# Odd mixer of a two-layer trunk: decay differences and masked U on GpSimd, four gate rows for three

## The chip, the cores and the metric

The kernel runs on one core of a Trainium2 chip, in one launch. The metric is the device time of one execution in microseconds (us). TensorE is PE (PEld its weight loads), VectorE is DVE, ScalarE is ACT, GpSimd is POOL, and SyncE (SP) only issues transfers.

## The reference

One inference step of a two-layer trunk for a prompt of 512 tokens and a sample group of 8 sequences of 4 tokens, width 1024, fp32. Each layer is a half-step FFN, a mixer and another half-step FFN. The mixer of the second (odd) layer is a gated DeltaNet with 8 heads of 128; the change lies in it alone:

```
def deltanet_mixer(u, conv_buf, S0, w_in, conv_w, A_log, dt_bias, o_gain, w_out):
    proj = u @ w_in
    qkv, z, b_logit, a_logit = jnp.split(proj, ...)
    qkv, new_buf = causal_conv(conv_buf, qkv, conv_w)
    q, k, v = jnp.split(jax.nn.silu(qkv), 3, axis=-1)      # q and k are l2-normalized per head
    g = -jnp.exp(A_log) * jax.nn.softplus(a_logit + dt_bias)
    o, S = gated_delta_chunked(q, k, v, beta, g, S0)
    o = rms_norm(o, o_gain) * jax.nn.silu(z)
    return o @ w_out, (new_buf, S)

# in gated_delta_chunked
    G = jnp.cumsum(gc, axis=-1)
    decay = jnp.exp(jnp.where(incl, G[..., :, None] - G[..., None, :], -jnp.inf))
    A = jnp.where(strict, jnp.einsum('bnhcd,bnhsd->bnhcs', kc, kc) * decay, 0.0) * bc[..., None]
```

Then a triangular solve with A, and a scan over the chunks that carries the state S.

## The kernel before

Activations are kept transposed, 128 rows by 544 columns (512 prompt, 32 sample) per tile. Every linear is written by `mm3`: weights and activations are each split in a high and a low part, three products for each of 8 blocks, so 24 matmuls into one PSUM tile `lin` for each half of the columns (256 and 288). In the odd mixer `lin` has two buffers, so PE can be two tiles ahead of the instruction that reads the first one back, which for all of them is one on DVE. A weight block is loaded by SP (`raw`), its high part made on ACT (`wh`, L328) and its low part on DVE (`wl`, L329).

The mixer works on its heads in four groups of two (0 and 1, 2 and 3, 4 and 5, 6 and 7). A string of tokens gives the order in which the pieces are written out, and a scheduler orders each engine's instructions from there; every engine then runs its list strictly in that order. The pieces that matter here:

- **Decays** (`head_decay`): the row G of a head is spread over all partitions by a transfer (`grow` for the first head of a group, the shared tile `xsq` for the second), then `Dn` and `Dt` are made by a subtraction of G per partition and a clamp against a constant mask (L1165, L1166: one DVE instruction per tile and chunk of 128, 16 for a group), and ACT takes the exponentials.
- **Head stage** (`head_stage`): two convolved projections (`conv_tile`: `lin` to `XP` by DVE at L1120, L1123 and L1124, the history columns of XP by POOL, then three DVE instructions `acc` L1134), squares and norms, products. POOL makes `qg` (L1214).
- **Solve**: 62 short DVE instructions `ltmp` (L1251) and `LT` (L1252), each needing the one before.
- **Chain** (`chain`): four chunk steps on PE, ACT and DVE, then `finish`: the norm `fo` by a dozen short DVE instructions (L984 to L989), ACT scales `ot` (L1328), PE transposes it (L1331), DVE multiplies it onto the gate row `sz` (L1335) and splits the result to `y` (L376).
- **Gate** (`gate`): one `mm3` into a row tagged `sz`, read back by DVE at L1565; three rows, one for each head in flight, each free again when `y` is split.
- **Sample state** (`sample_state`): for two heads and two halves of the sequences, `um` is U times a 0/1 mask of each sequence (four ACT instructions, L1518, into one buffer), a matmul `s` (L1520) and four DVE updates of S (L1523).

Rows tagged `st` (15 of them) hold Dn, Dt, kt, qg and vb of the heads in flight. `E.junk` are two scratch tiles for the elementwise result of squares whose sum alone is wanted. The constants `c_tri`, `c_stri` and `c_sones` are loaded once and used in `odd_setup` alone.

Of the kernel before, what the change touches and what calls it, by code (L numbers as in the profile page):

```python
# [7 lines left out]
F32 = mybir.dt.float32  # L8
# [4 lines left out]
ALU = mybir.AluOpType  # L13
# [983 lines left out]
def odd_consts(E, op):  # L997
    nc, I = E.nc, E.I

    def const(key, shape):  # L1000
        t = op.tile(shape, F32, name=key)
        nc.sync.dma_start(out=t, in_=I[key])
        return t
    E.tri = const("c_tri", [P, P])
    E.mba = const("c_mba", [P, P])
    E.mbp = const("c_mbp", [P, P])
    E.stri = const("c_stri", [NS, NS])
    E.sones = const("c_sones", [NS, NS])
    E.smba = const("c_smba", [NS, NS])
    E.smbp = const("c_smbp", [NS, NS])  # L1010
    E.bsel = const("c_bsel", [96, DB])

    rows = E.f(P)[:96]
    nc.sync.dma_start(out=rows, in_=I["dn_conv_w"].rearrange("a i (k p) -> (a i k) p", p=P))
    ps = E.m([P, 96])
    nc.tensor.transpose(ps, rows, E.ident[:96, :96])
    E.cw = op.tile([P, 96], F32, name="cw")
    nc.vector.tensor_copy(E.cw, ps)
    E.cst = op.tile([P, 24, 27], F32, name="dncst")
    cv = I["state_dn_conv"].rearrange("a b i c -> (a b i) c")  # L1020
    for g in range(6):
        st = E.f()
        nc.sync.dma_start(out=st[:24, :512], in_=cv[:, g * 512:(g + 1) * 512])
        ps = E.m([P, 4, 24])
        for j in range(4):
            nc.tensor.transpose(ps[:, j], st[:24, j * P:(j + 1) * P], E.ident[:24, :24])
        nc.vector.tensor_copy(E.cst[:, 4 * g:4 * g + 4, 3:], ps)
    gc = op.tile([P, 1], F32, name="ogain")
    nc.sync.dma_start(out=gc, in_=I["dn_o_gain"].rearrange("a p -> p a"))
    E.ogain = gc  # L1030
    E.ad = op.tile([P, 2, NH], F32, name="ad")
    nc.sync.dma_start(out=E.ad[:, 0], in_=I["dn_A_log"].to_broadcast([P, NH]))
    nc.sync.dma_start(out=E.ad[:, 1], in_=I["dn_dt_bias"].to_broadcast([P, NH]))


def odd_setup(E, op, sp, w_in):
# [5 lines left out]
    def ev(h, c0, cn, ps):  # L1042
        nc.vector.tensor_tensor(bt[:16, c0:c0 + cn], ps[:16], E.rstd[:16, c0:c0 + cn], op=ALU.mult)
    mm3(E, [w], E.xh, E.xl, ev)
    ps = E.m([P, 5, 16])
    for t, (c0, n) in enumerate(TOKS):
# [22 lines left out]
    gf = g[:, :4].rearrange("p a b -> p (a b)")  # L1069
    nc.tensor.matmul(ps[:, 0:32], lhsT=E.tri, rhs=gf, start=True, stop=True)  # L1070
    nc.tensor.matmul(ps[:, 32:64], lhsT=E.ones, rhs=gf, start=True, stop=True)
    nc.tensor.matmul(ps[:NS, 64:72], lhsT=E.stri, rhs=g[:NS, 4], start=True, stop=True)
    nc.tensor.matmul(ps[:NS, 72:80], lhsT=E.sones, rhs=g[:NS, 4], start=True, stop=True)
    nc.tensor.matmul(ps[:, 96:160], lhsT=E.ones[:NS], rhs=gm.rearrange("p a b -> p (a b)"), start=True, stop=True)
# [81 lines left out]
def head_decay(E, op, h):  # L1156
# [5 lines left out]
    Dt = op.tile([P, 4, P], F32, tag="st", name=E.nm("Dt"), bufs=ST)  # L1162
    for c in range(4):
        g = E.G[:, c, h:h + 1]
# [9 lines left out]
def head_stage(E, op, w_in, h, H, ssq, adr, sq):  # L1174
# [5 lines left out]
    kT = conv_tile(E, op, w_in, 1, h, sq)  # L1180
    ssk = op.tile([P, 4], F32, tag="ssk", name=E.nm("ssk"), bufs=2)
    pq = E.m([P, 4, P])
    for c in range(4):
        nc.tensor.transpose(pq[:, c], ch(qT)[:, c], E.ident)
    for c in range(4):
        nc.scalar.activation(E.junk[0], pq[:, c], AF.Square, accum_out=ssq[:, gi, c:c + 1])
    kt = op.tile([P, 4, P], F32, tag="st", name=E.nm("kt"), bufs=ST)
    pk = E.m([P, 4, P])
    for c in range(4):
        nc.tensor.transpose(pk[:, c], ch(kT)[:, c], E.ident)  # L1190
    for c in range(4):
        nc.scalar.activation(E.junk[0], pk[:, c], AF.Square, accum_out=ssk[:, c:c + 1])
    nc.scalar.activation(kt, pk, AF.Copy)
# [115 lines left out]
def chain(E, op, Hs, V, g0, ssq, sz, yy, cuts=(4,)):  # L1309
# [29 lines left out]
    for c in range(4):  # L1339
# [22 lines left out]
        for h in hs:  # L1362
            nc.scalar.activation(E.junk[1], ot[:, c, h], AF.Square, accum_out=sso[:, h, c:c + 1])
        S = Sn
# [31 lines left out]
def sample_group(E, op, sq, dec, g0, sz, yy):  # L1396
# [11 lines left out]
    kt, vt = kv[:, 0], kv[:, 1]  # L1408
    ssk = op.tile([NS, GH], F32, tag="sssk", name=E.nm("ssk"))
    for h in hs:  # L1410
        nc.scalar.activation(E.junk[1][:NS], kt[:, h], AF.Square, accum_out=ssk[:, h:h + 1])
    nc.vector.tensor_scalar(ssk, ssk, EPS, None, op0=ALU.add)
# [30 lines left out]
    nc.vector.tensor_tensor(V, pv, IB, op=ALU.add)  # L1443
    kw = R(P, "kw")
    nc.vector.tensor_tensor(kw, kt, bc(kwf, P), op=ALU.mult)
# [65 lines left out]
def sample_state(E, op, g0, S0, k3, ur):  # L1511
    nc, O = E.nc, E.O
    sp = lambda shape: cps(E, shape, "s")
    for h in range(GH):
        for q in range(2):
            um = op.tile([96, 4, P], F32R, tag="um", name=E.nm("um"))
            for b in range(4):
                nc.scalar.activation(um[:, b], ur[:, h].bitcast(F32), AF.Copy, scale=E.bsel[:, 4 * q + b:4 * q + b + 1])  # L1518
            ps = sp([P, 4, P])
# [7 lines left out]
def odd_mixer(E, cp, w_in, w_out, nxt):  # L1527
    nc, tc = E.nc, E.tc
    with E.phase(0, 2), tc.tile_pool(name=E.nm("oddw"), bufs=1) as op, tc.tile_pool(name=E.nm("odram"), bufs=1, space=bass.MemoryType.DRAM) as dp:
        E.dp, E.op = dp, op  # L1530
        E.ft, E.rt = (op, "acc", XW, 4), (op, "y", YB)
        E.junk = [op.tile([P, P], F32, name=f"junk{i}") for i in range(2)]
        norm_stats(E)
# [4 lines left out]
def odd_heads(E, op, dp, w_in, w_out, nxt):  # L1538
# [18 lines left out]
    def gate(h):  # L1557
        H = st[h // GH * GH]
        E.table("silu_and_others")
        z = op.tile([P, NT], F32, tag="sz", name=E.nm("sz"), bufs=3)  # L1560
        H.sz = getattr(H, "sz", []) + [z]
# [133 lines left out]
```

## Time and profile before

| what | value |
|---|---|
| median of 3 runs | 1911.97 us (1911.93 to 1913.39) |
| profiled execution | 1916.94 us, span 1915.2 us, mean granted clock 0.991 |
| busy: PE, PEld, DVE, ACT, POOL | 97%, 94%, 56%, 44%, 6% of the span |
| odd mixer | about 1198 to 1627 us of the span |

The profiled execution is 4.97 us longer than the median, and its span 1.74 us shorter than itself. Busy shares are means over stages: the odd mixer is read by itself below.

### The profile page before, as it was taken

To read this page: it belongs to the slowest core of one execution; us is meant where nothing else is said; L and a number is where in the kernel's file an instruction comes from. 1 tells how busy PE (TensorE), PEld (TensorE's weight loads), DVE (VectorE), ACT (ScalarE), POOL (GpSimd) and SP (SyncE) were. 2 spreads that over 40 slices of the span, in tenths; PEclk is the share of its full clock that TensorE was granted. 3 is DMA by queue.
4 is the path that set the end of the run, shared out by engine and by line. 5 is a ranking of instruction groups with operands and counts; after the bars stand their busy time and mean duration, and the time that the engine had idled before them with its cause. 6 is when DMAs were issued, how large, how long until landed. Compare 5 with 4: busy or idle time off the path is not lost.

```text
span 1915.2 us, 36694 instructions
## 1 busy us (share of the span) xinstructions
PE 1861.2 (97%) x15101; PEld 1793.0 (94%) x15101; DVE 1078.1 (56%) x2565; ACT 836.9 (44%) x1733; POOL 121.2 (6%) x229
## 2 busy tenths in 40 slices
PE   7999999999999999999999999899998999999999
PEld 6999999889777999999999999799997998999998
DVE  7444335776856444433544433688978877444422
ACT  6333224777755333323333322466675646333221
POOL 0000002111430000000000000111111100000000
PEclk9999999999999999999999999899999999999999
DMA  4323333222431333333332322333343332333232
GB/s 131 86 85 89 87 89 99 76 59 76 141 100 58 89 89 89 89 89 93 90 87 86 88 81 80 87 88 95 99 124 76 94 95 65 89 88 86 81 112 68
DMA packets 315973, 171.05 MB, mean 89 GB/s; under 512 B 28470, under 2 KB 310278, under 8 KB 315804
## 3 DMA queue, kind: packets, MB, share of 16 engines
q1 hardware_dynamic: 313244, 160.30, 29.5%
q0 software_dynamic: 2560, 8.39, 1.5%
q8 instruction: 119, 1.95, 0.4%
q14 instruction: 50, 0.41, 0.1%
HBM read 158.01 MB, written 10.65 MB: 88 GB/s over the span
## 4 chain that ended last, share of the span: by engine, by line
PE 58%; DVE 5%; ACT 2%; issue 1%; DMA 1%; POOL 0%; SPq 0%; ACTq 0%; DVEq 0%; POOLq 0%
PE lin L367 18%; PE lin L368 17%; PE lin L369 17%; DVE acc L1134 1%; DVE wl L329 1%; DVE LT L1252 1%; DVE ltmp L1251 1%; PE s L1479 0%; DMA raw<-in_w_in_odd 0%; PE m L1211 0%; DMA raw<-in_w_ffn_in 0%; ACT wh L328 0%; DVE Dn L1165 0%; PE c L1349 0%; DMA grs<-gdr 0%
## 5 line engine op out<-in xcount | busy, mean ns | idle before, releaser
L367 PE MATMUL lin<-xh,wh 128*128 128x256 f32 (+2 forms) x2992 | 875.0, 293 | 20.0 <-DVE XP L1120 5.0
L368 PE MATMUL lin<-xl,wh 128*128 128x256 f32 (+2 forms) x2992 | 870.5, 291 | 1.4 <-DVE xl L376 0.7
L369 PE MATMUL lin<-xh,wl 128*128 128x256 f32 (+2 forms) x2992 | 865.8, 290 | 0.5 <-DVE wl L329 0.5
L367 PEld LDWEIGHTS lin<-xh,wh 128*128 128x128 f32 (+1 forms) x2992 | 565.6, 189 | 25.7 <-ACT wh L328 6.4
L368 PEld LDWEIGHTS lin<-xl,wh 128*128 128x128 f32 (+1 forms) x2992 | 566.1, 189 | 3.9 <-DVE xl L273 1.5
L369 PEld LDWEIGHTS lin<-xh,wl 128*128 128x128 f32 (+1 forms) x2992 | 566.8, 189 | 2.6 <-issue 0.8
L328 ACT ACTIVATE wh<-raw 128x1024 fp32r<-128x1024 f32 x261 | 275.8, 1057 | 492.1 <-PE lin L368 419.2
L329 DVE TENSOR_TENSOR wl<-raw,wh 128x1024 fp32r<-128x1024 f32 x261 | 317.2, 1215 | 89.9 <-PE lin L369 88.0
L367 PE MATMUL lin<-hh,wh 128*128 128x288 f32 (+1 forms) x1024 | 295.7, 289 | 0.0
L368 PE MATMUL lin<-hl,wh 128*128 128x288 f32 (+1 forms) x1024 | 295.4, 288 | 0.0
L369 PE MATMUL lin<-hh,wl 128*128 128x288 f32 (+1 forms) x1024 | 294.9, 288 | 0.0
L368 PEld LDWEIGHTS lin<-hl,wh 128*128 128x128 f32 x1024 | 193.0, 188 | 0.2
L369 PEld LDWEIGHTS lin<-hh,wl 128*128 128x128 f32 x1024 | 192.7, 188 | 0.1
L367 PEld LDWEIGHTS lin<-hh,wh 128*128 128x128 f32 x1024 | 192.5, 188 | 0.1
L406 DVE TENSOR_TENSOR sg<-lin,rstd 128x256 f32<-128x256 f32 (+1 forms) x128 | 55.9, 438 | 162.1 <-PE lin L369 162.1
L375 ACT ACTIVATE hh<-pr 128x256 fp32r<-128x256 f32 (+1 forms) x128 | 55.1, 431 | 204.1 <-DVE pr L412 203.9
L411 DVE TENSOR_TENSOR pr<-lin,rstd 128x256 f32<-128x256 f32 (+1 forms) x128 | 56.5, 441 | 155.2 <-PE lin L369 155.1
L428 DVE SCALAR_TENSOR_TENSOR x<-lin,x 128x256 f32<-128x256 f32 x64 | 28.2, 441 | 168.7 <-PE lin L369 168.7
L376 DVE TENSOR_TENSOR hl<-pr,hh 128x256 fp32r<-128x256 f32 (+1 forms) x128 | 56.6, 442 | 61.2 <-ACT hh L375 61.2
L100 ACT ACTIVATE sg<-sg 128x256 f32<-128x256 f32 (+1 forms) x128 | 53.7, 422 | 55.9 <-DVE sg L406 55.9
L272 ACT ACTIVATE xh<-x,vec 128x544 fp32r<-128x544 f32 (+2 forms) x64 | 39.6, 631 | 71.5 <-DVE x L428 59.3
L1134 DVE SCALAR_TENSOR_TENSOR acc<-XP,cw,acc 128x568 f32<-128x568 f32 x72 | 58.8, 817 | 2.5 <-ACT acc L1132 2.2
(492 smaller groups left out, 2068.7 us busy)
## 6 DMA issues: line engine op xcount, KB each, us to landing
raw<-in_w_ffn_in SPq DMA_DIRECT2D x128, 512.0 KB
raw<-in_w_ffn_out SPq DMA_DIRECT2D x64, 512.0 KB
raw<-in_w_in_odd SPq DMA_DIRECT2D x32, 512.0 KB
raw<-in_w_in_even SPq DMA_DIRECT2D x20, 512.0 KB
raw<-in_w_out_even SPq DMA_DIRECT2D x8, 512.0 KB
S<-in_state_dn_S SPq DMA_DIRECT2D x8, 512.0 KB
out_dn_S_sample<-S SPq DMA_DIRECT2D x8, 512.0 KB
raw<-in_w_out_odd SPq DMA_DIRECT2D x8, 512.0 KB
```

What stands on the lines that cost most here:

```text
L100: i = self.nc.scalar.activation(out, in_, func, **kw).ins
L272: nc.scalar.activation(xh, x, AF.Copy, scale=g)
L328: nc.scalar.activation(self.h, raw, AF.Copy)
L329: nc.vector.tensor_tensor(self.l, raw, self.h.bitcast(F32), op=ALU.subtract)
L367: nc.tensor.matmul(ps[:n], lhsT=wh, rhs=rh, start=(i == 0), stop=False)
L368: nc.tensor.matmul(ps[:n], lhsT=wh, rhs=rl, start=False, stop=False)
L369: E.last_mm = nc.tensor.matmul(ps[:n], lhsT=wl, rhs=rh, start=False, stop=(i == len(terms) - 1)).ins
L375: nc.scalar.activation(yh, src, AF.Copy)
L376: nc.vector.tensor_tensor(yl, src, yh.bitcast(F32), op=ALU.subtract)
L406: nc.vector.tensor_tensor(s, ps, E.rstd[:, c0:c0 + cn], op=ALU.mult)
L411: nc.vector.tensor_tensor(p_, ps, E.rstd[:, c0:c0 + cn], op=ALU.mult)
L1134: nc.vector.scalar_tensor_tensor(a, XP[:, j:j + XW - 3], cw[j], a, op0=ALU.mult, op1=ALU.add)
```

## The change

- For the heads from 2 on, Dn and Dt are made on POOL: a subtraction of a broadcast G and an addition of a broadcast mask, each over 128x512, four instructions for a head in place of eight on DVE. Heads 0 and 1 stay as they were.
- `um` is one POOL instruction over 96x512 in place of four on ACT.
- The tag `sz` has four rows.
- The scratch tiles are gone: squares write into `kt`, `vb` or `kw`, tiles that are rewritten or no longer read; `kt` of a head and `kw` of the sample are therefore allocated earlier.
- The three constants are loaded in `odd_setup`, by three transfers of SP into a tile tagged `acc`.

```diff
@@ -1001,11 +1001,8 @@
         t = op.tile(shape, F32, name=key)
         nc.sync.dma_start(out=t, in_=I[key])
         return t
-    E.tri = const("c_tri", [P, P])
     E.mba = const("c_mba", [P, P])
     E.mbp = const("c_mbp", [P, P])
-    E.stri = const("c_stri", [NS, NS])
-    E.sones = const("c_sones", [NS, NS])
     E.smba = const("c_smba", [NS, NS])
     E.smbp = const("c_smbp", [NS, NS])
     E.bsel = const("c_bsel", [96, DB])
@@ -1042,6 +1039,10 @@
     def ev(h, c0, cn, ps):
         nc.vector.tensor_tensor(bt[:16, c0:c0 + cn], ps[:16], E.rstd[:16, c0:c0 + cn], op=ALU.mult)
     mm3(E, [w], E.xh, E.xl, ev)
+    cst = E.f()
+    tri, stri, sones = cst[:, :P], cst[:NS, P:P + NS], cst[:NS, P + NS:P + 2 * NS]
+    for t, key in ((tri, "c_tri"), (stri, "c_stri"), (sones, "c_sones")):
+        nc.sync.dma_start(out=t, in_=E.I[key])
     ps = E.m([P, 5, 16])
     for t, (c0, n) in enumerate(TOKS):
         nc.tensor.transpose(ps[:n, t], bt[:16, c0:c0 + n], E.ident[:16, :16])
@@ -1067,10 +1068,10 @@
     nc.vector.tensor_tensor(gm, g[:NS, 4:5].to_broadcast([NS, DB, NH]), bc(E.bsel[:NS], NH), op=ALU.mult)
     ps = E.m([P, 160])
     gf = g[:, :4].rearrange("p a b -> p (a b)")
-    nc.tensor.matmul(ps[:, 0:32], lhsT=E.tri, rhs=gf, start=True, stop=True)
+    nc.tensor.matmul(ps[:, 0:32], lhsT=tri, rhs=gf, start=True, stop=True)
     nc.tensor.matmul(ps[:, 32:64], lhsT=E.ones, rhs=gf, start=True, stop=True)
-    nc.tensor.matmul(ps[:NS, 64:72], lhsT=E.stri, rhs=g[:NS, 4], start=True, stop=True)
-    nc.tensor.matmul(ps[:NS, 72:80], lhsT=E.sones, rhs=g[:NS, 4], start=True, stop=True)
+    nc.tensor.matmul(ps[:NS, 64:72], lhsT=stri, rhs=g[:NS, 4], start=True, stop=True)
+    nc.tensor.matmul(ps[:NS, 72:80], lhsT=sones, rhs=g[:NS, 4], start=True, stop=True)
     nc.tensor.matmul(ps[:, 96:160], lhsT=E.ones[:NS], rhs=gm.rearrange("p a b -> p (a b)"), start=True, stop=True)
     E.G = op.tile([P, 5, NH], F32, name="G")
     nc.vector.memset(E.G, 0.0)
@@ -1160,7 +1161,12 @@
     nc.sync.dma_start(out=grow, in_=E.gdr[h:h + 1].to_broadcast([P, NT]))
     Dn = op.tile([P, 4, P], F32, tag="st", name=E.nm("Dn"), bufs=ST)
     Dt = op.tile([P, 4, P], F32, tag="st", name=E.nm("Dt"), bufs=ST)
-    for c in range(4):
+    if h >= GH:
+        gb = bc(E.G[:, :4, h], P)
+        for d, m in ((Dn, E.mba), (Dt, E.mbp)):
+            nc.gpsimd.tensor_tensor(d, ch(grow), gb, op=ALU.subtract)
+            nc.gpsimd.tensor_tensor(d, d, m.unsqueeze(1).to_broadcast([P, 4, P]), op=ALU.add)
+    for c in range(4 if h < GH else 0):
         g = E.G[:, c, h:h + 1]
         nc.vector.scalar_tensor_tensor(Dn[:, c], ch(grow)[:, c], g, E.mba, op0=ALU.subtract, op1=ALU.max)
         nc.vector.scalar_tensor_tensor(Dt[:, c], ch(grow)[:, c], g, E.mbp, op0=ALU.subtract, op1=ALU.min)
@@ -1179,17 +1185,17 @@
     qT = conv_tile(E, op, w_in, 0, h, sq)
     kT = conv_tile(E, op, w_in, 1, h, sq)
     ssk = op.tile([P, 4], F32, tag="ssk", name=E.nm("ssk"), bufs=2)
+    kt = op.tile([P, 4, P], F32, tag="st", name=E.nm("kt"), bufs=ST)
     pq = E.m([P, 4, P])
     for c in range(4):
         nc.tensor.transpose(pq[:, c], ch(qT)[:, c], E.ident)
     for c in range(4):
-        nc.scalar.activation(E.junk[0], pq[:, c], AF.Square, accum_out=ssq[:, gi, c:c + 1])
-    kt = op.tile([P, 4, P], F32, tag="st", name=E.nm("kt"), bufs=ST)
+        nc.scalar.activation(kt[:, c], pq[:, c], AF.Square, accum_out=ssq[:, gi, c:c + 1])
     pk = E.m([P, 4, P])
     for c in range(4):
         nc.tensor.transpose(pk[:, c], ch(kT)[:, c], E.ident)
     for c in range(4):
-        nc.scalar.activation(E.junk[0], pk[:, c], AF.Square, accum_out=ssk[:, c:c + 1])
+        nc.scalar.activation(kt[:, c], pk[:, c], AF.Square, accum_out=ssk[:, c:c + 1])
     nc.scalar.activation(kt, pk, AF.Copy)
     nc.vector.tensor_scalar(ssk, ssk, EPS, None, op0=ALU.add)
     cf = op.tile([P, 4, 4], F32, tag="cf", name=E.nm("cf"), bufs=4)
@@ -1360,7 +1366,7 @@
             nc.tensor.matmul(po[:, h], lhsT=Hs[h].PT[:, c], rhs=U[:, h], start=(c == 0), stop=True)
         nc.scalar.activation(ot[:, c], po, AF.Copy)
         for h in hs:
-            nc.scalar.activation(E.junk[1], ot[:, c, h], AF.Square, accum_out=sso[:, h, c:c + 1])
+            nc.scalar.activation(Hs[h].vb[:, c], ot[:, c, h], AF.Square, accum_out=sso[:, h, c:c + 1])
         S = Sn
         if c in cuts:
             finish(c - 4 // len(cuts), c)
@@ -1407,8 +1413,9 @@
     nc.scalar.activation(kv, ps, AF.Copy)
     kt, vt = kv[:, 0], kv[:, 1]
     ssk = op.tile([NS, GH], F32, tag="sssk", name=E.nm("ssk"))
+    kw = R(P, "kw")
     for h in hs:
-        nc.scalar.activation(E.junk[1][:NS], kt[:, h], AF.Square, accum_out=ssk[:, h:h + 1])
+        nc.scalar.activation(kw[:, h], kt[:, h], AF.Square, accum_out=ssk[:, h:h + 1])
     nc.vector.tensor_scalar(ssk, ssk, EPS, None, op0=ALU.add)
     cf = op.tile([NS, 4, GH], F32, tag="scf", name=E.nm("scf"))
     rk, rb, rb2, kwf = cf[:, 0], cf[:, 1], cf[:, 2], cf[:, 3]
@@ -1441,7 +1448,6 @@
         nc.tensor.matmul(pv[:, h], lhsT=A2[:, h], rhs=IB[:, h], start=True, stop=True)
     V = R(NS, "V")
     nc.vector.tensor_tensor(V, pv, IB, op=ALU.add)
-    kw = R(P, "kw")
     nc.vector.tensor_tensor(kw, kt, bc(kwf, P), op=ALU.mult)
     k3 = op.tile([96, GH, P], F32R, tag="k3", name=E.nm("k3"))
     for h in hs:
@@ -1514,8 +1520,7 @@
     for h in range(GH):
         for q in range(2):
             um = op.tile([96, 4, P], F32R, tag="um", name=E.nm("um"))
-            for b in range(4):
-                nc.scalar.activation(um[:, b], ur[:, h].bitcast(F32), AF.Copy, scale=E.bsel[:, 4 * q + b:4 * q + b + 1])
+            nc.gpsimd.tensor_tensor(um, ur[:, h].bitcast(F32).unsqueeze(1).to_broadcast([96, 4, P]), bc(E.bsel[:, 4 * q:4 * q + 4], P), op=ALU.mult)
             ps = sp([P, 4, P])
             nc.tensor.matmul(ps, lhsT=k3[:, h], rhs=um, start=True, stop=True)
             s = S0[h][:, 4 * q:4 * q + 4]
@@ -1529,7 +1534,6 @@
     with E.phase(0, 2), tc.tile_pool(name=E.nm("oddw"), bufs=1) as op, tc.tile_pool(name=E.nm("odram"), bufs=1, space=bass.MemoryType.DRAM) as dp:
         E.dp, E.op = dp, op
         E.ft, E.rt = (op, "acc", XW, 4), (op, "y", YB)
-        E.junk = [op.tile([P, P], F32, name=f"junk{i}") for i in range(2)]
         norm_stats(E)
         odd_setup(E, cp, op, w_in)
         odd_heads(E, op, dp, w_in, w_out, nxt)
@@ -1557,7 +1561,7 @@
     def gate(h):
         H = st[h // GH * GH]
         E.table("silu_and_others")
-        z = op.tile([P, NT], F32, tag="sz", name=E.nm("sz"), bufs=3)
+        z = op.tile([P, NT], F32, tag="sz", name=E.nm("sz"), bufs=4)
         H.sz = getattr(H, "sz", []) + [z]
         w = W(E, w_in[:, 3072 + h * P:3072 + (h + 1) * P])
 
```

In all, POOL has 40 instructions more (24 for the decays, 16 for `um`), DVE 48 fewer, ACT 64 fewer.

POOL's list where the decays of heads 2 and 3 are made. `XP` and `dncst` are history columns of the convolutions, `k` belongs to the sample. Before:

```order
L1127 COPY dncst<-XP_13787 128x3 [waits DVE_49]
L1128 COPY dncst<-XP_13787 128x24 [waits DVE_49]
L1115 MEMSET XP_14631 128x3 [waits DVE_49,Activation_49,Pool_49]
L1116 COPY XP_14631<-dncst 128x8x3
L1452 COPY k_1747_14226<-k_1747_14226 32x256 [waits Activation_49,Pool_49]
L1127 COPY dncst<-XP_14560 128x3 [waits DVE_49,Pool_49]
L1128 COPY dncst<-XP_14560 128x24 [waits DVE_49]
```

And now:

```order
L1128 COPY dncst<-XP_13783 128x3 [waits DVE_49]
L1129 COPY dncst<-XP_13783 128x24 [waits DVE_49]
L1116 MEMSET XP_14607 128x3 [waits DVE_49,Activation_49,Pool_49]
L1117 COPY XP_14607<-dncst 128x8x3
L1167 TENSOR_TENSOR Dn_14510<-grow_14508,G 128x512 [waits DMAHW5_49]
L1167 TENSOR_TENSOR Dt_14511<-grow_14508,G 128x512
L1168 TENSOR_TENSOR Dn_14510<-Dn_14510,c_mba 128x512 [waits Pool_49]
L1168 TENSOR_TENSOR Dt_14511<-Dt_14511,c_mbp 128x512 [waits Pool_49]
L1167 TENSOR_TENSOR Dn_14520<-xsq,G 128x512 [waits DMAHW7_49]
L1167 TENSOR_TENSOR Dt_14521<-xsq,G 128x512
L1168 TENSOR_TENSOR Dn_14520<-Dn_14520,c_mba 128x512 [waits Pool_49]
L1168 TENSOR_TENSOR Dt_14521<-Dt_14521,c_mbp 128x512 [waits Pool_49]
```

Eight instructions stand ahead of the history copies of the next projection, and no other engine's result stands between them but the two transfers of G.

DVE's list around the first read-back of the gate row of head 5 (`sz_16595` before, `sz_16543` now; `y_15485` and `y_15487` are the results of heads 2 and 3). Before:

```order
L1335 SCALAR_TENSOR_TENSOR sz_15199<-c_15774,ogain,sz_15199 128x512 [waits PE_49]
L376 TENSOR_TENSOR y_15485<-sz_15138,y_15484 128x512 [waits Activation_49]
L1134 SCALAR_TENSOR_TENSOR acc_16503<-XP_16445,cw,acc_16503 128x568 [waits Activation_49,Pool_49]
L376 TENSOR_TENSOR y_15487<-sz_15199,y_15486 128x512 [waits Activation_49]
L1134 SCALAR_TENSOR_TENSOR acc_16503<-XP_16445,cw,acc_16503 128x568 [waits DVE_49]
L1251 TENSOR_TENSOR ltmp_16522<-LA_16520,LT_16521 128x66
L1134 SCALAR_TENSOR_TENSOR acc_16503<-XP_16445,cw,acc_16503 128x568 [waits DVE_49]
L1252 TENSOR_TENSOR LT_16521<-LT_16521,ltmp_16522 128x22x3 [waits DVE_49]
L1565 TENSOR_TENSOR sz_16595<-lin_16602,rstd 128x256
L1251 TENSOR_TENSOR ltmp_16522<-LA_16520,LT_16521 128x63 [waits DVE_49]
```

And now:

```order
L1260 COPY LA_15236<-LT_15237 128x256 [waits DVE_49]
L1569 TENSOR_TENSOR sz_16326<-lin_16360,rstd 128x288 [waits PE_49]
L329 TENSOR_TENSOR wl_16547<-raw_16544,wh_16546 128x1024 [waits DMAHW0_49]
L1121 TENSOR_TENSOR XP_16393<-lin_16396,rstd 128x256 [waits PE_49,Pool_49]
L1124 TENSOR_TENSOR XP_16393<-lin_16422,rstd 128x256 [waits PE_49]
L1125 TENSOR_TENSOR XP_16393<-lin_16422,rstd 128x8x4
L329 TENSOR_TENSOR wl_16607<-raw_16604,wh_16606 128x1024 [waits DMAHW5_49,Activation_49]
L1283 COPY lv_15312<-c_15319 32x8x32 [waits PE_49]
L1569 TENSOR_TENSOR sz_16543<-lin_16550,rstd 128x256 [waits PE_49]
L1291 COPY lv_15312<-c_15347 32x8x32 [waits PE_49]
```

The gate of head 5 was read back behind the split that frees its row; now it stands among the products of the solve of heads 2 and 3 (`lv`, `V`), ahead of their chain, and its second half follows 55 rows later. On PE the gate's 48 matmuls moved with it: between the last product of that chain (L1360) and the first transposition of its `finish` (L1331) stood 58 matmuls of `lin`, and now stand 40; behind them comes the next group's projection, whose first read-back on DVE stands right behind `fo`.

## Rows read from the trace of the kernel before

**Rows 1.** Stretches: length, busy PE, PEld, DVE, ACT, POOL (instructions), clock, DMA share, GB/s.
```profile
1198.00:1627.00 429.00, 407.41 (x3774) 380.61 (x3772) 347.95 (x1220) 265.48 (x754) 60.93 (x128) 0.97 0.34 91
1275.00:1300.00 25.00, 24.32 (x196) 22.54 (x193) 22.65 (x101) 18.17 (x48) 2.78 (x9) 1.00 0.32 86
1325.00:1350.00 25.00, 24.99 (x211) 24.10 (x209) 23.44 (x93) 23.28 (x84) 4.95 (x9) 1.00 0.46 123
1350.00:1375.00 25.00, 23.73 (x192) 23.08 (x192) 24.07 (x89) 18.29 (x44) 5.21 (x11) 1.00 0.35 96
1425.00:1450.00 25.00, 19.03 (x136) 18.14 (x134) 21.66 (x78) 18.61 (x47) 4.47 (x9) 0.88 0.35 95
```

**Rows 2.** Timeline of PE, 1428 to 1446 us: start, duration, engine, line, operation.
```profile
1428.68 0.39 PE L1360 MATMUL pv<-U,Dt 128*128 128x128 f32 x2
...
1437.38 0.33 PE L1331 MATMUL c<-ident,ot 128*128 128x128 f32 x1 [0.85 <-ACT ot L1328]
...
1440.99 0.27 PE L1405 MATMUL s<-ident,sq 128*32 128x128 f32 x1
1445.78 0.58 PE L367 MATMUL lin<-xh,wh 128*128 128x256 f32 x1 [4.51 <-DVE sz L1565]
```

**Rows 3.** Busy time by engine in 5 us behind that wait.
```profile
1445.00:1450.00 5.00, 4.22 (x20) 4.22 (x20) 4.69 (x17) 2.56 (x8) 0.25 (x2) 0.50 0.17 44
```

**Rows 4.** Timeline of DVE, 1430 to 1446 us.
```profile
1430.40 0.17 DVE L1375 SCALAR_TENSOR_TENSOR sso<-sso,ssq 128x8 f32<-128x8 f32 x1
1431.52 0.35 DVE L1165 SCALAR_TENSOR_TENSOR Dn<-xsq,G,c_mba 128x128 f32<-128x128 f32 x1 [0.96 <-DMA xsq<-gdr]
...
1436.23 0.16 DVE L989 SCALAR_TENSOR_TENSOR fo<-rsa,rsy 128x8 f32<-128x8 f32 x1
...
1442.99 0.68 DVE L376 TENSOR_TENSOR y<-sz,y 128x512 fp32r<-128x512 f32 x1
...
1445.31 0.41 DVE L1565 TENSOR_TENSOR sz<-lin,rstd 128x256 f32<-128x256 f32 x1
```

**Rows 5.** Timeline of PE: two waits, at 1282 and at 1369 us.
```profile
1282.61 0.21 PE L1430 MATMUL s<-ident,sA 32*32 32x32 f32 x2 [0.60 <-DVE ltmp L1251]
...
1369.81 0.39 PE L367 MATMUL lin<-xh,wh 128*128 128x256 f32 x1 [1.27 <-DVE XP L1120]
```

**Rows 6.** Timeline of DVE: two of the decay differences of heads 2 and 3.
```profile
1267.06 0.34 DVE L1165 SCALAR_TENSOR_TENSOR Dn<-grow,G,c_mba 128x128 f32<-128x128 f32 x1
1267.32 0.35 DVE L1166 SCALAR_TENSOR_TENSOR Dt<-grow,G,c_mbp 128x128 f32<-128x128 f32 x1
```

**Rows 7.** Instructions of line 1214: minimum/median/maximum ns, first and last start.
```profile
L1214 POOL TENSOR_TENSOR qg<-acc,grow x4: 1287/1290/1294, 1236.0 to 1503.2; 128x512 f32<-128x512 f32 x4
L1214 POOL TENSOR_TENSOR qg<-acc,xsq x4: 1297/1328/1609, 1254.0 to 1523.1; 128x512 f32<-128x512 f32 x4
```

**Rows 8.** Page, costliest groups: mean ns of one, idle time before them.
```profile
L329 DVE TENSOR_TENSOR wl<-raw,wh 128x1024 fp32r<-128x1024 f32 x261 | 317.2, 1215 | 89.9 <-PE lin L369 88.0
...
L1134 DVE SCALAR_TENSOR_TENSOR acc<-XP,cw,acc 128x568 f32<-128x568 f32 x72 | 58.8, 817 | 2.5 <-ACT acc L1132 2.2
```

**Rows 9.** Timeline of DVE beside three instructions of line 1214.
```profile
1254.04 2.68 DVE L1134 SCALAR_TENSOR_TENSOR acc<-XP,cw,acc 128x568 f32<-128x568 f32 x2 [0.22 <-ACT acc L1132]
...
1503.88 1.73 DVE L329 TENSOR_TENSOR wl<-raw,wh 128x1024 fp32r<-128x1024 f32 x1
...
1523.37 1.21 DVE L1252 TENSOR_TENSOR LT<-LT,ltmp 128x63 f32<-128x63 f32 x1
...
1524.86 0.22 DVE L1252 TENSOR_TENSOR LT<-LT,ltmp 128x60 f32<-128x60 f32 x1
```

**Rows 10.** Instructions of line 1489: minimum/median/maximum ns.
```profile
L1489 DVE TENSOR_TENSOR Ur<-Us,Ur x4: 406/417/1419, 1324.9 to 1562.6; 32x256 fp32r<-32x256 f32 x4
```

**Rows 11.** POOL timeline, 1277 to 1285 us.
```profile
1284.06 0.19 POOL L1127 COPY dncst<-XP 128x3 f32<-128x3 f32 x1 [6.15 <-DVE XP L1123]
```

**Rows 12.** Timeline of ACT: four instructions of line 1518.
```profile
1411.61 1.28 ACT L1518 ACTIVATE um<-Ur,c_bsel 96x128 fp32r<-96x128 f32 x4 [0.35 <-PE s L1520]
```

## Prediction

> **What bounds the kernel now.** I read the busy time by stretches first. Over the odd mixer, 429 us, PE is busy 407.41 us and DVE 347.95 us, so PE sets the time and can lose at most some 21 us to waits; but DVE has little slack in places: 22.65 of 25 us from 1275, 23.44 from 1325, 24.07 from 1350 [rows 1]. One stretch stands out: from 1425 to 1450 PE is busy only 19.03 us, at a mean clock of 0.88.
>
> The timeline of PE shows why. The chain of heads 2 and 3 ends with the product at 1428.68. Filler (the gate of head 5 among it) covers the norm on the other engines until a wait of 0.85 us for `ot` at 1437.38; then PE sits idle 4.51 us, from 1440.99 to 1445.78, until DVE has read back the gate tile `sz` [rows 2]. Behind that wait the granted clock is 0.50: 20 matmuls in 5 us [rows 3], against 196 in 25 us, or 39 in 5, at full clock [rows 1].
>
> DVE's timeline shows what the read-back waited for. The norm starts at 1430.40 and gives `fo` only at 1436.23, with one group's decay differences between its short instructions, one of which waits 0.96 us for its transfer. The split to `y` at 1442.99 ends at 1443.67 and frees the third gate row; the read-back, some instructions behind, runs at 1445.31 [rows 4]. So PE waits for a row, the row for the chain's end, and the chain's end for a DVE that also makes decay differences.
>
> Two smaller waits show where DVE sets PE's pace elsewhere: 0.60 us at 1282.61 (a sample product) and 1.27 us at 1369.81 (a read-back of XP) [rows 5].
>
> **The change part by part.** *Four gate rows.* The gate of head 5 now takes a row that nobody holds, and its read-back stands ahead of the chain. The wait of 4.51 us goes: **-4.5**. The slow clock began in that wait and held on behind it; the 4.22 us that PE was busy at 0.50 would be 2.1 at full clock: **-2.1**. Another slow stretch could come of another wait, so this term lies between 0 and -2.1; I take all of it, since the rows show the clock low right behind this wait.
>
> *What is late next.* The gate was also filler. Between the chain's last product and the first transposition PE now has 40 matmuls, not 58; at 196 in 25 us that is 5.1 us. Before, `fo` came 7.55 us after the chain's last product began (1428.68 to 1436.23) and the transposition 1.15 us later. Of those, eight decay differences at 0.26 us, their spacing [rows 6], and the wait of 0.96 us leave DVE: some 3.0 us. So `ot` would be ready about 5.7 us after the product, and PE would wait 0.6 us where it waited 0.85: **0**, if nothing new holds DVE there (second rival).
>
> *Decays on POOL.* DVE loses 48 instructions at 0.26 us, 12.5 us, or 4.2 for a group. POOL gets 24 instructions over 128x512 with two inputs in SBUF. The nearest rows are those of `qg`, the same shape: 1.29 to 1.33 us in the median [rows 7], so 10.3 us for the eight of a group. The price that matters is what such an instruction does to DVE. `qg` ran eight times. Four times a DVE instruction that began beside it took longer: two `acc` 2.68 us where two take 1.63 by the mean of 817 ns, a `wl` 1.73 where the mean is 1.215, an `LT` 1.21 where its like takes 0.22 [rows 8, 9], a `Ur` 1.42 where the median is 0.417 [rows 10]. That is 1.05 + 0.51 + 0.99 + 1.00 = 3.55 us. The other four I count as nothing: 0.45 us for each on average, between 0 and 1.05. At 0.45 the eight of a group hold DVE 3.6 us and spare it 4.2. I take the average, because DVE's list around these eight is mixed as it was around `qg` (read-backs from PSUM, weights, short SBUF instructions), and call the result **0** rather than a small gain.
>
> The Trainium skill, in "SBUF — State Buffer", section "SBUF: two separate sides", says that GpSimd and a DVE instruction with two SBUF inputs take an exclusive lock on one pair of ports, and the other is fully blocked for the whole instruction. The four long rows agree with it; that the other four cost nothing means that DVE did not ask for the ports then. By the rule with DVE always asking, the estimate would be 24 x 1.29 - 12.5, or 18.5 us more on DVE.
>
> Behind these eight on POOL stand the history copies that free XP. For heads 2 and 3 the first of them ran at 1284.06, after 6.15 us of idle time [rows 11]. DVE began its differences there at 1267.06 [rows 6]; eight on POOL from then end at 1277.4 at the earliest, so 6.7 us of waiting for the ports are hidden, and beyond that a read-back into XP waits.
>
> *Masked U on POOL.* Four ACT instructions take 1.28 us together [rows 12], one on POOL about 1.29 by `qg`, so the way from U to the matmul is as long as it was. ACT gets back 16 x 1.28, 20 us, but no wait above is for ACT's throughput: 0. Against that stand 16 more instructions that may hold DVE, 1.8 us for a group at 0.45. Around the first group's, PE is busy 24.99 of 25 us, so little shows at once; DVE, at 23.44, carries its lateness into the next stretch, where PE already waits for it. I count about half of one group's: **+1.0**, between 0 and 7.2.
>
> *Scratch and constants.* A square into another tile costs what it cost. Three small loads (72 KB in all) leave on SP ahead of a weight block and are wanted only after a projection and its transposes; the nearest row of a transfer that came late is the 0.96 us of rows 4, so 0, at most +1.
>
> **Sum.** -4.5 - 2.1 + 0 + 0 + 1.0 = **-5.6 us**. The profiled execution (1916.94 us) would come out at 1911.3; the median of the runs is 4.97 us lower, 1911.97, and would become **1906.4**.
>
> **The rivals.** *The port costs more than the rows saved (slower).* Eight instructions stand in a row on POOL, where `qg` was single, and DVE's solve, norm and sample work is made of short instructions on SBUF. If each holds DVE 1.05 us, as the longest did, DVE loses 24 x 1.05 - 12.5 = 12.7 us at places where it has 1 to 3 us of slack in 25 and PE already waits for it; -6.6 + 12.7 + 1.0 is +7.1: 1919.1. It decides from a hold of 0.75 us each (24 x 0.75 = 12.5 + 5.6), and from 0.91 the kernel is slower by more than 0.2%. For it speak DVE's busy shares; against it, that half of the rows of `qg` cost nothing, and that at the third group DVE also gets rid of a wait for a transfer. The rule cited above is this rival at its worst. Chance 0.30.
>
> *The finish takes the place of the gate row (no change).* The eight of heads 6 and 7 fall into the norm of heads 2 and 3, as DVE's did. If they hold it 3.6 us, `ot` is ready 9.3 us after the chain's last product, PE with 5.1 us of filler waits 4.2 where it waited 0.85, and so long a wait may bring the slow clock back. Then -4.5 + 3.4 + 1.0 is -0.1: 1911.9. For it speaks that `fo` stands ahead of the next read-back on DVE, so PE cannot run further ahead than two tiles; against it, that the transfer for the second head delays half of the eight past the norm. Chance 0.24.
>
> *DVE's relief shows (more).* If the holds mostly miss, the waits of 0.60, 1.27 and 0.85 us go as well: 2.7 more and no +1.0, 1902.7. Chance 0.10.
>
> *The gates wait as before* is not open as a way to no change: with four rows, the row for head 5 is free from the first chain on.
>
> **How the numbers follow.** The forecast has 0.36, with DVE's relief faster: 0.46. About 0.2% (3.8 us) is what a measurement of this kernel can tell from no change. The range reaches to 1919 for the holds at their longest and to 1901 for the full relief with a little over; I leave about 1 in 10 above it, for holds nearer the whole 1.29 us, and less below. The forecast's own range is 1902 to 1908.
>
> **What would show it.** In the profile after: no wait of PE for `sz` and no slow clock behind it near 1440; a wait for `ot` there under 2 us; DVE busy about as before in the stretches where POOL makes decays. Long rows among DVE's short ones (`LT`, `ltmp`, `rsa` at over 1 us) beside L1167 and L1168 in numbers near 24, a longer wait at the sample product near 1282 and at the XP read-back near 1369, would show the first rival; a PE wait of 3 us or more for `ot` or the next read-back, the second. The prediction falls if a hold costs DVE more than 0.75 us on average, or if the freed wait reappears at the finish.

## The result and the profile after

The changed kernel takes **1961.2 us** in the median of 6 runs, where the kernel before took 1912.6 beside it: a ratio of **1.0257** (95% interval 1.0231 to 1.0282). It is 48.6 us slower. The prediction, 1906.4 us and faster, was wrong, and the time lies beyond the rival that ends on the slower side too.

The page of the profiled execution after (1976.1 us, the slowest of the six and 15 us above the median; its mean granted clock is 0.970, that of the others 0.973 to 0.982): the span, busy time by engine, and the granted clock in 40 slices.

```profile
span 1974.3 us, 36622 instructions
...
PE 1895.4 (96%) x15101; PEld 1821.6 (92%) x15101; DVE 1083.4 (55%) x2517; ACT 813.4 (41%) x1669; POOL 175.1 (9%) x269
...
PEclk9999999999999999999999999989998878999999
```

All the loss is in the odd mixer: there the clock falls to 8 and 7 tenths. PE is still "96% busy", which misleads, since matmuls at half clock count as busy twice as long (20 in 5 us against 39, as the prediction read them from [rows 3] and [rows 1]). The stretches after, in the columns of [rows 1] (the mixer, the stretch of the finish of heads 2 and 3, and one behind it):

```profile
1198.00:1690.00 492.00, 444.84 (x3798) 412.44 (x3797) 356.69 (x1179) 244.58 (x694) 114.34 (x168) 0.89 0.31 80
...
1450.00:1475.00 25.00, 17.39 (x122) 16.61 (x122) 20.97 (x51) 12.31 (x38) 15.63 (x17) 0.86 0.38 107
...
1525.00:1550.00 25.00, 25.00 (x294) 22.47 (x295) 14.42 (x48) 8.39 (x32) 6.06 (x6) 0.59 0.13 34
```

PE's idle time in the mixer grew from 21.6 us (429 less 407.41) to 47.2, and the mean clock fell from 0.97 to 0.89. Where PE waited, from its timeline (the bracket is the idle time before the instruction and what ended it):

```profile
1282.81 0.21 PE L1437 MATMUL s<-ident,sA 32*32 32x32 f32 x2 [2.79 <-DVE ltmp L1257]
...
1373.52 0.32 PE L1428 MATMUL s<-sq 128*32 128x32 f32 x2 [4.60 <-ACT skv L1413]
...
1467.17 0.47 PE L1337 MATMUL c<-ident,ot 128*128 128x128 f32 x1 [7.28 <-ACT ot L1334]
...
1493.90 0.21 PE L1437 MATMUL s<-ident,sA 32*32 32x32 f32 x2 [2.06 <-DVE ltmp L1257]
...
1524.90 0.32 PE L1485 MATMUL s<-S,wqz 128*32 128x128 f32 x4 [2.83 <-DMA S<-in_state_dn_S]
```

The wait of 4.51 us for the gate tile [rows 2] is gone, as forecast. But the finish of heads 2 and 3 now waits 7.28 us for `ot`, the sample products near 1282 wait 2.79 where they waited 0.60 [rows 5], and others are new. Around the end of each of these five waits the granted clock falls to 0.5, for 6.8 to 20.5 us; in all the mixer of this execution has 105.8 us at half clock, where it had 23.9 before.

What made `ot` late shows on DVE and POOL side by side. POOL's timeline, the decay differences of heads 6 and 7 (four of eight), then DVE's, the norm of heads 2 and 3:

```profile
1457.11 1.05 POOL L1167 TENSOR_TENSOR Dt<-grow,G 128x512 f32<-128x512 f32 x1
1458.12 1.29 POOL L1168 TENSOR_TENSOR Dn<-Dn,c_mba 128x512 f32<-128x512 f32 x1
...
1460.61 1.05 POOL L1167 TENSOR_TENSOR Dn<-xsq,G 128x512 f32<-128x512 f32 x1
1461.62 1.05 POOL L1167 TENSOR_TENSOR Dt<-xsq,G 128x512 f32<-128x512 f32 x1
```

```profile
1456.16 1.01 DVE L1381 SCALAR_TENSOR_TENSOR sso<-sso,ssq 128x8 f32<-128x8 f32 x1
...
1457.21 0.98 DVE L984 TENSOR_SCALAR rsi<-sso 128x8 int32<-128x8 int32 x1
...
1458.22 1.22 DVE L985 TENSOR_SCALAR rsy<-rsi 128x8 int32<-128x8 int32 x1
...
1460.70 0.97 DVE L988 SCALAR_TENSOR_TENSOR rsa<-rsa,sso 128x8 f32<-128x8 f32 x1
...
1461.71 0.97 DVE L989 SCALAR_TENSOR_TENSOR rsy<-rsa,rsy 128x8 f32<-128x8 f32 x1
...
1466.40 0.15 DVE L989 SCALAR_TENSOR_TENSOR fo<-rsa,rsy 128x8 f32<-128x8 f32 x1
```

An instruction on 8 elements a row, 0.16 us by [rows 4], takes 0.97 to 1.22 us: it ends where a POOL instruction ends, and the next pair does the same. The time that a DVE instruction beside a POOL instruction lasts longer than the same instruction does elsewhere is called its hold from here on. The norm, from `sso` to `fo`, takes 10.2 us where it took 5.8 with DVE's own differences in it [rows 4].

### The profile page after: what moved, and what is told of

The parts are those of the page before. It is cut to its first block, busy times and chain, and to the rows that moved or that the text cites. A ratio compares the mean times of both kernels' runs of the same rounds, so it can differ in the third digit from the quotient of the medians.

```text
span 1974.3 us, 36622 instructions
## 1 busy us (share of the span) xinstructions
PE 1895.4 (96%) x15101; PEld 1821.6 (92%) x15101; DVE 1083.4 (55%) x2517; ACT 813.4 (41%) x1669; POOL 175.1 (9%) x269
## 4 chain that ended last, share of the span: by engine, by line
PE 58%; DVE 6%; ACT 2%; DMA 2%; issue 1%; SPq 0%; DVEq 0%; ACTq 0%
PE lin L367 18%; PE lin L368 17%; PE lin L369 17%; DVE acc L1135 1%; DMA S<-in_state_dn_S 1%; PE s L1485 1%; DVE wl L329 1%; DMA raw<-in_w_in_odd 1%; PE c L1355 0%; DMA tdr<-LA 0%; DVE ltmp L1257 0%; DVE LT L1258 0%; DVE rsa L987 0%; PE m L1217 0%; DVE rsa L988 0%
```

## The experiments

Ratios are to the kernel before, run beside each kernel on the same chip, with 95% intervals. The list of an engine is the order of its instructions in the program.

**Theories.** *The holds*: the loss is DVE waiting while POOL's 40 new instructions read and write, and PE waiting for DVE, with the slow clock behind. *The order*: the edits that cost nothing by themselves (scratch rows, room for the row) place instructions anew on every engine, and the new lists are worse. *The row*: the fourth gate row itself only moves a wait.

**1. The change in halves.** `e1_rows` is the change without both moves to POOL; `e4_room` is that with three gate rows. `e2_decays` and `e3_um` are the kernel before with one move each.

> The change without its two moves to GpSimd: decays on VectorE, masked U on ScalarE, four gate rows, scratch rows and held constants given up. Theory A (ports: GpSimd's instructions hold VectorE's short ones, as in the norm of heads 2 and 3 where a dozen of them took about 1 us each): nothing is left to hold, so 1905 to 1913 us. Theory B (order: giving up the scratch rows and constants rearranges the lists of all engines, so that PE loses its filler and its clock): most of the 49 us stays, 1935 us or more.

> As the run with four gate rows, but with three: only the scratch rows and the held constants are given up. The lists of the two differ in a handful of places, at the gate of head 5. If the fourth row is worth what the wait of 4.5 us and the slow clock behind it promised, this one is about 6 us slower than the other; if the row was not what set that wait, both are within 2 us. Theory A: about 1912. Theory B: 1935 or more, as the other.

> The kernel before with one part of the change: the later groups' decay differences on GpSimd. Theory A: the 24 instructions hold VectorE some 18 us in the trace of the change, for 12.5 us of instructions saved, and most of it in front of PE; with the slow clock that follows waits, 1930 to 1950 us. Theory B: the lists move less, 1908 to 1918 us.

> The kernel before with the masked U alone on GpSimd: 16 instructions that held VectorE some 8 us in the trace of the change, in stretches where PE is nearly full. Theory A: 1914 to 1922 us. Theory B: 1910 to 1914 us.

| kernel | median us | ratio |
|---|---|---|
| e1_rows | 1922.1 | 1.0050 [1.0032, 1.0068] |
| e4_room | 1926.6 | 1.0068 [1.0046, 1.0089] |
| e2_decays | 1925.6 | 1.0052 [1.0034, 1.0071] |
| e3_um | 1926.5 | 1.0060 [1.0043, 1.0077] |

Every part is slower alone. No single story holds all: the scratch and room edits (e4), priced at nothing, cost 12.7 us, as much as either move. `e1` and `e4` differ by the fourth row alone: 4.5 us in the medians, but their intervals overlap.

**2. The same lists with nothing to read.** `e7` has the decays on POOL as memsets, `e8` the masked U, so that these are not computed; the lists of PE and DVE are those of e2 and e3. `e9` does it to the whole change; its list of DVE differs from the change's in 345 of 2517 places. From e9 (cut):

```
-            nc.gpsimd.tensor_tensor(d, ch(grow), gb, op=ALU.subtract)
-            nc.gpsimd.tensor_tensor(d, d, m.unsqueeze(1).to_broadcast([P, 4, P]), op=ALU.add)
...
+            nc.gpsimd.memset(d.rearrange("p a b -> p (a b)").bitcast(H16), 0.5)
+            nc.gpsimd.memset(d.rearrange("p a b -> p (a b)").bitcast(H16), 0.25)
```

> As the run with the later groups' decays on GpSimd alone, but each of the 24 GpSimd instructions is a memset of the same tile, written as 1024 16-bit values so that it lasts about 1 us too; it reads nothing from SBUF. The decays of heads 2 to 7 are left out by it. The lists of PE and VectorE are the same, instruction by instruction. Theory A (ports): the 17 us that VectorE was held in that run go, the waits of PE at the sample product and at the chain's end with them; 1906 to 1916 us. Theory B (the lists' new order, or ScalarE's exponentials waiting for a slow GpSimd): 1920 us or more, as that run.

> As the run with the masked U alone on GpSimd, with a memset of the same tile in place of each of its 16 instructions: the sample's state update is left out by it. The lists of PE, VectorE and ScalarE are the same. Theory A: the 6 us of holds were in front of PE; 1912 to 1918 us. Theory B (the order that follows from the move): 1922 us or more.

> The whole change with memsets for all 40 of its GpSimd instructions (later decays and the sample's state update left out). PE's list differs from the change's in 3% of its places. Theory A: of the 49 us, what the ports cost goes, waits and slow clock together, and what the scratch rows cost stays: 1920 to 1932 us. Theory B: 1945 us or more.

e7 gives 1912.5 us, 0.9992 [0.9980, 1.0003]: the decays' whole loss goes. A memset does not wait for the transfer of G either, but in e2 none of POOL's 24 instructions had stood idle for it by more than 0.3 us. e8 gives 1920.4, 1.0030 [1.0019, 1.0041]: half of the masked U's loss stays. The solve of heads 0 and 1 on DVE beside POOL, which makes the decays of heads 2 and 3, first in e2, then in e7:

```profile
1272.23 1.29 POOL L1167 TENSOR_TENSOR Dt<-Dt,c_mbp 128x512 f32<-128x512 f32 x1
1273.48 1.05 POOL L1166 TENSOR_TENSOR Dn<-xsq,G 128x512 f32<-128x512 f32 x1
...
1272.56 1.00 DVE L1256 TENSOR_TENSOR ltmp<-LA,LT 128x31 f32<-128x31 f32 x1
1273.60 1.00 DVE L1257 TENSOR_TENSOR LT<-LT,ltmp 128x31 f32<-128x31 f32 x1
1274.64 0.95 DVE L1256 TENSOR_TENSOR ltmp<-LA,LT 128x30 f32<-128x30 f32 x1
```

```profile
1273.93 0.95 POOL L1165 MEMSET Dt<- 128x1024 bf16 x1
...
1274.01 0.20 DVE L1255 TENSOR_TENSOR ltmp<-LA,LT 128x31 f32<-128x31 f32 x1
1274.25 0.23 DVE L1256 TENSOR_TENSOR LT<-LT,ltmp 128x31 f32<-128x31 f32 x1
1274.51 0.20 DVE L1255 TENSOR_TENSOR ltmp<-LA,LT 128x30 f32<-128x30 f32 x1
```

Each 0.2 us step of the solve becomes 1.0 beside an instruction that reads, and stays 0.2 beside a memset of 0.95. At the finish, PE in e2 waits 3.90 us for `ot`; in e7 no wait for `ot` is over 0.5 us.

```profile
1440.61 0.33 PE L1336 MATMUL c<-ident,ot 128*128 128x128 f32 x1 [3.90 <-ACT ot L1333]
```

But e9 takes 1943.6, 1.0151 [1.0129, 1.0174], so memsets are no clean control. POOL's, DVE's and PE's timelines of e9 at the finish:

```profile
1443.92 0.94 POOL L1166 MEMSET Dt<- 128x1024 bf16 x1
...
1449.28 0.94 POOL L1167 MEMSET Dt<- 128x1024 bf16 x1
```

```profile
1444.11 6.14 DVE L984 TENSOR_SCALAR rsi<-sso 128x8 int32<-128x8 int32 x1
```

```profile
1453.59 0.48 PE L1336 MATMUL c<-ident,ot 128*128 128x128 f32 x1 [5.98 <-ACT ot L1333]
```

One `rsi`, 0.16 us elsewhere, ended only when the last of seven memsets back to back did. It has one input, unlike the steps of the solve. Twice more in e9 such an instruction (`rsy` of L985, 0.17 us elsewhere) took 0.82 us beside a single memset; instructions with two inputs lasted longer beside a memset only where they stood behind one of these three. So:

**3. Short memsets.** `e11` is the whole change with memsets of 32 and 96 of each 128 columns for the decays' pairs and one for the masked U.

> The whole change with GpSimd's 40 instructions made short: two memsets of parts of the tile in place of a subtraction and an addition, one for a masked U (later decays and the sample's state update left out). Lists as in the run with long memsets. In that run a one-input VectorE instruction of the norm stood 6.1 us beside seven memsets in a row, so memsets of 1 us were no clean test. Theory A (what is left of the 49 us is GpSimd holding VectorE): 1915 to 1928 us, near the run with the scratch rows given up alone. Theory B (what is left is the new order of the lists): 1938 us or more, as with the long memsets.

1931.8 us, 1.0110 [1.0089, 1.0131]. POOL's memsets hold DVE about 1 us in all here. So some 29 us of the 48.6 go with the length and the reads of POOL's instructions, and some 18 stay.

**4. The row and the constants.** `e10` is the kernel before with a fourth gate row, room for it found without touching the order of the squares (constants loaded in the setup, the scratch rows in an unused half of a constant). `e5` loads the constants in the setup alone.

> The kernel before with the fourth gate row and nothing else of the change that moves work: the room comes from the three constants and from scratch that lies in half of a tile of ones no longer read, so squares stay where they were written out. The prediction's own term: the wait of 4.5 us for the gate row and the slow clock behind it go, 1906 us (-6.6). Rival: the finish is what PE waits for next, 1911 to 1914 us.

> The kernel before with the three constants loaded in the setup: all lists but SP's are as before. If a late transfer there costs time, 1915 us or more; if it is hidden, as forecast, 1912 to 1914, which also shows how far equal lists agree.

e10: 1917.2 us, 1.0021 [1.0009, 1.0032]. PE's timeline where it waited 4.51:

```profile
1439.69 0.40 PE L367 MATMUL lin<-xh,wh 128*128 128x288 f32 x1 [1.65 <-DVE sz L1566]
```

The wait shrinks to 1.65 us (for DVE's read-back of `sz`) and the clock stays at full there, yet at the end of another wait come 10.2 us of half clock:

```profile
1564.42 0.38 PE L1299 MATMUL c<-V,Dn 64*64 64x64 f32 x3 [1.54 <-DVE lv L1296]
```

What the row saves at its place comes back in other waits: over the mixer PE is idle 23.5 us, where it was 21.6 before. (This profile, at 1914.9 us, is of one of the fastest of ten executions, so it shows less than the median's loss of 3.3 us.) e5: 1912.0, 0.9993 [0.9983, 1.0004]: constants cost nothing.

**5. Smaller pieces.** `e12` cuts the decays of e2 into 96 instructions of 128 columns.

> The kernel before with the later groups' decays on GpSimd in pieces of 128 columns, as VectorE had them: 96 instructions, same work, same lists on PE, VectorE and ScalarE as the run with 24. Theory A (a VectorE instruction is held until the GpSimd instruction that has the ports ends): a short one now waits a third of a microsecond and not a whole one, so much of the 11.7 us comes back, 1914 to 1919 us. Rival (the ports are taken as often as GpSimd has an instruction, and four times as many cost as much in all): 1922 us or more.

1930.7 us, 1.0085 [1.0062, 1.0109]: no better than e2, if anything worse. Yet the holds fell, from 13.4 us in e2 to 8.6, and PE's wait for `ot` from 3.90 to 0.60. In return POOL needs 14.5 to 15.4 us for the decays of a group, where it needed 10.0 to 10.9, and PE has a new wait of 4.53 us for `wh` at 1455. How far the one brings the other was not tested.

**6. Which scratch edit.** `e13` makes one edit alone: the squares of q and k go into `kt`, claimed earlier. `e15` makes the two others (into `vb` and `kw`). `e18` moves the squares of k only:

```
-  nc.scalar.activation(E.junk[0], pk[:, c], AF.Square, accum_out=ssk[:, c:c + 1])
+  nc.scalar.activation(kt[:, c], pk[:, c], AF.Square, accum_out=ssk[:, c:c + 1])
```

> The kernel before with one part of the scratch given up: the squares of q and k go to kt, which is allocated earlier. This alone gives all lists a new order (half of VectorE's places). Theory C (the order is what the scratch rows cost, whichever of them is given up): 1918 to 1930 us, like all of them. Rival (it is the chain's or the sample's scratch): 1911 to 1915.

> The kernel before with two of the scratch edits alone: the squares of the heads' outputs into vb, the sample's k squares into kw, which is claimed earlier; the squares of q and k still go to the scratch row. If the scratch's price is the q and k squares' tile, claimed earlier (e13), it is the kernel before: 1912 to 1915 us. If any new order of the lists costs, it is slower too: 1918 to 1927.

> The kernel before with one line changed: the squares of k go into kt, which stands where it stood, those of q to the scratch row. If any untying of a square from the row brings the list that costs, it gives e13's price, a ratio of 1.011. If it needs the q squares, which stand ahead of it in the list, it is the kernel before, 0.998 to 1.003.

| kernel | median us | ratio |
|---|---|---|
| e13_kt | 1935.5 | 1.0114 [1.0096, 1.0133] |
| e15_vb_kw | 1919.1 (before: 1918.1) | 1.0011 [0.9997, 1.0025] |
| e18_k_only | 1927.0 (before: 1918.6) | 1.0064 [1.0037, 1.0091] |

The squares of q and k are the price; those of k alone bring about half. Claiming the tile earlier, without the squares, leaves the list of every engine as it was. DVE's list in e13 differs from before in 992 of 2565 places, all of them in the odd mixer. But e15, which costs nothing that can be told, differs in 587: a new order is not by itself the price. New waits of e13, from PE's timeline, for the sample's state, whose load now lands too late, beside the wait for the gate tile that it still has:

```profile
1445.41 0.58 PE L367 MATMUL lin<-xh,wh 128*128 128x256 f32 x1 [3.23 <-DVE sz L1565]
...
1494.55 0.64 PE L1479 MATMUL s<-S,wqz 128*32 128x128 f32 x16 [1.84 <-DMA S<-in_state_dn_S]
...
1578.33 0.86 PE L1479 MATMUL s<-S,wqz 128*32 128x128 f32 x24 [1.47 <-DMA S<-in_state_dn_S]
```

**7. Do the parts add up?** `e14` is the whole change with the scratch rows kept (in the unused half of a constant), `e17` is e14 with memsets, `e20` the whole change with only the squares of q and k back on a scratch row.

> The whole change, but the squares still go to two scratch rows (kept in an unused half of a constant), so that all that is left out is the scratch rows' giving up. If the parts add up, it costs the decays' 11.7, the masked U's 12.6 and the fourth row's 3: about 1940 us, some 21 below the change, and the scratch rows' new order is the rest. If the two moves to GpSimd are worse together than apart, whatever the scratch does, it comes out near the change itself: 1955 to 1961.

> The kernel of e14_scratch_kept, but GpSimd's 40 instructions (decays and masked U) are memsets of the same tiles that read nothing (1024 x 16 bit, some 0.94 us each): the decays and the masked U aren't computed. If the two moves cost by what they hold and by the masked U's new order alone, it gives 1912.6 + 6.4 (e8) + 3 (fourth row) = about 1920 us, or 1915 without the row's. If the lists' order of both moves together is bad by itself, it stays above 1930.

> The whole change but one edit: the squares of q and k go to a scratch row, as before, in an unused half of a constant. If that edit is what the new order costs, it gives e14's time, a ratio of about 1.010 and some 1937 us, 24 below the change. If it is the two moves with any new order of the lists, it stays near the change, 1950 to 1961.

| kernel | median us (before: 1918.1; for e20 1918.6) | ratio |
|---|---|---|
| e14_scratch_kept | 1937.5 | 1.0102 [1.0079, 1.0125] |
| e17_kept_no_reads | 1919.6 | 1.0006 [0.9995, 1.0017] |
| e20_squares_kept | 1936.9 | 1.0104 [1.0078, 1.0131] |

e20 is the change with one edit undone, and it falls from 1.0257 to 1.0104: that edit is worth 1.5% of the time. e17 shows that the row and both moves, with new lists but nothing read, cost nothing that can be told; with the reads, e14, 1%. (The two lists of DVE differ in 369 of 2517 places, so this comparison is less clean than that of e2 and e7.) PE in e14 at the finish:

```profile
1447.42 0.47 PE L1337 MATMUL c<-ident,ot 128*128 128x128 f32 x1 [4.78 <-ACT ot L1334]
```

The finish is late again. In e17 no wait for `ot` is over 0.5 us, so it is the holds that make it late.

## Why the prediction was wrong

**The gate-row wait (-4.5): right at its place, but no gain.** The wait went in the change, and 1.65 us of it stayed in e10. Alone, with the term for the clock, the row was to give -6.6 us; e10 is 3.3 us slower than the kernel before.

**The slow clock behind it (-2.1): right there, wrong in sum.** It went at that place. In the change it came up behind five longer waits and others, 105.8 us for 23.9. In e10 one new stretch of 10.2 us came and the mixer has 17.1 us in all, but e5, whose lists on DVE and ACT are those of before, has 17.1 too: so much varies from one execution to the next. The prediction had said another wait could bring it back, and took the whole gain.

**Decays on POOL (0): the step that failed.** The prediction set an average hold against the DVE time that was spared, as if a hold cost the same wherever it falls. The average, 0.45 us from eight single `qg`, was too low: in the change 17 long DVE instructions stood beside the 24 of the decays, 14.7 us above the median of the same instructions before, **0.61 us** each (13.4 us and 0.56 in e2). (The expectations of e2 and e7 speak of 18 and 17 us; the traces give 14.7 and 13.4.) But 0.61 is under the 0.75 from which the first rival decides, and against the 12.5 us spared it would leave DVE only some 2 us worse. What decided is the place. The three groups of eight held DVE 4.8, 2.5 and 7.4 us; the 7.4 fall on eight instructions of one norm, each needing the one before, 0.93 us for each POOL instruction, where the prediction had 3.6 us, and PE waits for that norm. Alone the move costs 11.7 us (e2), with DVE held 13.4 us for 12.5 spared, and the loss goes when POOL reads nothing (e7). The Trainium skill, in "SBUF — State Buffer", section "SBUF: two separate sides", says that a GpSimd instruction that reads SBUF and a DVE instruction with two SBUF inputs exclude each other for a whole instruction; the estimate from that rule was 18.5 us more on DVE with DVE always asking. The rows agree with the exclusion (1.00 us beside a reading instruction in e2, 0.20 beside a memset in e7), and with an average toll of about half of a POOL instruction, 0.61 of some 1.2 us.

**What is late next (0, the finish): the second rival came.** It gave 4.2 us of wait for `ot`; it is 3.90 in e2, 4.78 in e14 and 7.28 in the change. Of the two signs by which the prediction was to fall, this one came and the average over 0.75 did not. The prediction let the two rivals exclude each other; they have one cause.

**Masked U (+1.0): too small.** 16 instructions of 1.08 us hold DVE 7.8 us in the change (0.49 each), and alone cost +12.6 us (e3), about half of it by the reads (e8).

**Scratch rows (0): the other step that failed.** "A square into another tile costs what it cost" holds for the square and not for the program. The squares of q and k share one row before, which ties them in their order; into `kt` they are free, and the lists come out otherwise. That they now wait for `kt` to become free is not what costs: ACT is idle 4.7 us before these squares in e13, and was 11.3 before. Alone that costs 1.0114 (e13), in the change 1.0257/1.0104, or 1.015. The whole change with short memsets, where POOL holds little, stands at 1.0110 (e11). The constants' 0 was right.

**The sum.** 1.0104 (e20: the row, both moves, the other scratch edits) times 1.0114 (e13) is 1.0219, of 1.0257 measured. The intervals of the three leave it open whether anything is missing: the parts add up within the noise.

**What stays open.** Why the lists with free squares are worse was not taken to a single instruction; that it is the order, and nothing else that the edit does, is argued and not shown. In the profiles the mixer of e13 is 17.8 us longer than before, with 8.6 us more of PE's idle time (5.4 of them in waits over 0.6 us) and 13.6 us more at half clock. Nor do the edits add simply: with the two other scratch edits beside it, and the constants, the same edit measures 1.0068 (e4). No version here that computes the whole result beats the kernel before; e5 and e15 are level with it.

## What to carry to other kernels

Before moving elementwise work to GpSimd, look at what DVE runs beside it, not at how busy DVE is: chains of short SBUF instructions (a solve, a reciprocal root) can pay the length of a GpSimd instruction at every link. Price the chain that the next engine waits for, not the sum over DVE. Cutting the GpSimd work into pieces shortened the holds here (e12) and still gained nothing. An edit that only changes where a result is thrown away can cost more than the edit that it makes room for, if it unties work that an automatic order places; measure it alone, before the rest. Where PE is the bound and waits are rare, allow for a half-clock stretch behind a new wait of 2 us or more: in the change all such waits of the mixer had one, in e2 one of 2.27 us had none.

## What the runs showed of the hardware

- DVE and POOL took turns, one for one: the first eight of a dozen dependent instructions on 8 elements each, 0.16 us by [rows 4], took 0.97 to 1.22 us beside eight POOL instructions, seven of them of 1.05 to 1.29 us. It goes both ways: POOL additions of 1.27 to 1.29 us took 2.27 and 2.28 beside a `wl` of DVE.
- Memsets, which read nothing, left the solve's two-input steps at 0.20 us (e7), but held DVE instructions with one input: in e9 two of 0.17 us took 0.82 beside one memset each, and one took 6.14 beside seven back to back. Why it was not let in between these seven was not found.
- A POOL subtraction over 128x512 with a broadcast column took 1.05 us, an addition 1.27 to 1.29, where DVE did not delay them; `qg`, the same shape, 1.29 to 1.33 [rows 7].
